# A two-layer decoder trunk: values first, the first weights loaded whole, and the forget gate's sums in six pieces

## The chip, the cores and the metric

The kernel runs on one core of a Trainium2 chip. Its engines are TensorE (PE, with weight loads listed apart as PEld), VectorE (DVE), ScalarE (ACT), GpSimd (POOL) and SyncE (SP), which here issues the DMAs. The metric is the device time of one execution in microseconds (us). Before the change it is 2600.77 us, the median of three runs (2596.73 to 2602.89).

## The reference

The input is 2048 tokens of width 1024, in float32. Layer A normalizes the tokens and projects them with one weight matrix of 4112 columns to q, k, v (1024 each), 16 forget logits and a gate. Cut to what matters here:

```python
u = rmsnorm(h, norm_a_g[i])
proj = u @ w_in_a[i]
q, k, v, f_logit, gate = jnp.split(proj, [...])
q = rmsnorm(q.reshape(b, s, 16, 64), qnorm_a_g[i])
k = rmsnorm(k.reshape(b, s, 16, 64), knorm_a_g[i])
log_f = jax.nn.log_sigmoid((f_logit + b_forget[i]).astype(jnp.float32))
c = jnp.cumsum(log_f, axis=1)
logits = q @ k.T * scale + c[query] - c[key]      # causal, per head
o = softmax(logits) @ v
h = h + (o * jax.nn.silu(gate)) @ w_out_a[i]
```

Layer B then computes one shared set of keys and values from h, projects its own q and gate, rotates 16 of 64 dimensions by angles that come from the token positions, attends in a window of 128 tokens, and adds its output projection. It is not touched by the change.

## The kernel before

Every float32 product is made of three matmuls: each operand is split into a high and a low part (`uh`, `ul` for the normed tokens, `wh`, `wl` for the weights), and high x high, high x low and low x high are summed in one accumulator. A token block is 128 tokens; with a contraction of 1024 = 8 x 128 a block and a group of columns take 24 matmuls, all on line 525.

Layer A's projections (`projections`) run over seven groups of columns, and within a group over 16 token blocks. The groups before are: q heads 0 to 5 with the 16 forget logits (400 columns), q heads 6 to 11 (384), k heads 0 to 7 and 8 to 15 (512 each), v heads 0 to 3 with q heads 12 to 15 (512), v heads 4 to 9 and 10 to 15 (384 each). The first group also norms the tokens (`norm`, `norm_transpose`: a load of x, squares on ACT, the reciprocal root on DVE, eight transposes on PE), two blocks ahead of their use. A block of q or k is then normed per head (`qk_norm`), transposed on PE a block or two later (`qk_transpose`), split, and stored for two blocks at a time. A block of v is split and stored at once (`v_tile`). The accumulators are three buffers `b2`; transposes use `pa` and `pb`.

A group's weights come by `weights`: four loads, each of two 128-row strips into one of two `wr` buffers, and eight splits (line 335 on ACT, line 336 on DVE) into nine buffers `wh` and nine `wl`. The x tiles of odd blocks use the same two `wr` buffers. The x tiles of even blocks, the stages of q and k, value tiles of over four heads and the gate-weight splits all take one of four buffers `st`.

Beside the blocks, 24 side jobs run, four to a group from the second group on (blocks 0, 3, 6, 9): 16 saves of the normed tokens to DRAM (`spill_u`, 1 MB each), then eight splits of the gate weights (`split_w`: a load of 512 KB, two splits, two stores; three `st` buffers). Attention needs both, since it computes the gate projection as filler between its own matmuls (line 785), with the saved tokens coming back through `wh` and `wl`. After its group, `forget` computes the log-sigmoid of the forget logits (exponential and logarithm on ACT), a running sum over all tokens (two matmuls, 15 small additions), and its transposed rows, stored as `ca`.

After the last group come the angle tables (`angles`, small operations on DVE and one sine on ACT) and attention. It goes head by head and, within a head, through four chunks of 512 queries. For each 128 queries it first finds row maxima (line 668, one or two pieces, each a matmul or two and a reduction on DVE), writes them by DMA as a row of the q operand, and then computes scores (lines 714, 715), exponentials on ACT, a high-low split on ACT and POOL, sums on DVE, and the product with v (line 755). The maxima of the next head are computed beside the scores of the current one; for the first head there is no earlier head to stand beside.

The program is written as loops, but the framework that builds it places each engine's instructions itself, by the readiness that it expects; the saves alone are held in program order. An engine, and SP with its DMA issues, then executes its list strictly in that order.

Of the kernel before, what the change touches and what calls it, by code (L numbers as in the profile page):

```python
# [21 lines left out]
P = 128  # L22
# [26 lines left out]
JOBS_AT = (0, 3, 6, 9)  # L49

# [22 lines left out]
class Trunk:  # L73
# [230 lines left out]
    def weights(self, src, c0, w, gain=None, extra=None, into=None):  # L304
# [9 lines left out]
        for dt in range(NDT):  # L314
            if dt % 2 == 0:
# [89 lines left out]
    def normer(self, src):  # L405
# [11 lines left out]
        def upto(n):  # L417
            while done[1] < min(n, NTB):
                while done[0] < min(done[1] + 2, NTB):
                    _, junk = parts(done[0])  # L420
                    ready.append(self.norm(src, done[0], junk))
                    done[0] += 1
                self.norm_transpose(ready.pop(0), *parts(done[1]))
# [4 lines left out]
    def projections(self, normed, groups, later=None, pre=None, hook=None):  # L428
# [7 lines left out]
        norm(1)  # L436
        if pre is not None:
            self.load_vectors(self.loads[:1])
        SW = 2 * P
        stages = {}  # L440
        z = None
# [13 lines left out]
        if later is not None:  # L455
# [23 lines left out]
            jobs = [  # L479
# [3 lines left out]
            jobs += [partial(split_w, dt) for dt in range(NDT)]  # L483

        for gi, grp in enumerate(groups):
            x2 = grp.get("extra")
            n = grp["n"] + (x2[1] if x2 else 0)
            W = self.weights(grp["w"], grp["c0"], grp["n"], grp["gain"], x2)
            if gi == 0:
                norm(2)  # L490
                if pre is not None:
                    pre()
# [24 lines left out]
            for tb in range(NTB):  # L517
                norm(tb + NORM_AHEAD)
                if gi and tb in JOBS_AT and jobs:
# [28 lines left out]
            if grp.get("forget"):  # L548
                self.forget(z)

    def forget(self, z):
# [3 lines left out]
        e, u = self.sb("sq", sh), self.sb("sq", sh)  # L555
        d, r = self.sb("qn", sh), self.sb("qn", sh)
# [10 lines left out]
        flat = r.rearrange("p t h -> p (t h)")  # L567
        inb, tot = self.ps("pa", sh), self.ps("pb", sh)
        nc.tensor.matmul(inb.rearrange("p t h -> p (t h)"), self.tri, flat, start=True, stop=True)
        nc.tensor.matmul(tot.rearrange("p t h -> p (t h)"), self.ones, flat, start=True, stop=True)  # L570
        nc.vector.memset(e[:, 0, :], 0.0)
        for tb in range(1, NTB):
            nc.vector.tensor_tensor(e[:, tb, :], tot[:, tb - 1, :], e[:, tb - 1, :], ALU.add)
        nc.vector.tensor_tensor(z, inb, e, ALU.add)
        sc = -float(HD) ** 0.5
        for ch in range(NCH):
            tr = self.ps(("pa", "pb")[ch % 2], [H, 4, P])
            for j in range(4):
                self.flip(tr[:, j, :], z[:, ch * 4 + j, :])
            trf = tr.rearrange("h j t -> h (j t)")  # L580
            hl = self.sb("st", [H, 2, CH])
# [609 lines left out]
```

## Time and profile before

| what | us |
|---|---|
| median of three runs | 2600.77 |
| the profiled execution | 2600.68 |
| its span in the trace | 2598.8 |
| first projection matmul | 11.7 |
| layer A's first group (400 columns, with the norms) | 11.7 to 114.1 |
| second group (384 columns, beside `forget`) | 114.1 to 195.3 |
| the two k groups | 195.3 to 387.9 |
| v with the last q heads | 387.9 to 479.7 |
| the two v groups | 479.7 to 616.1 |
| attention's first head | 616.1 to 699.3 |
| mean granted share of the TensorE clock | 0.983 |

A timeline row gives the start, the duration, the engine, the line, the operation, what it writes and reads, shapes and count, and in brackets the idle time of the engine ahead of it and what ended it. Matmuls are pipelined: a row's duration is longer than the distance to the next row, and the distance is what a stream of them costs. In a table of stretches a row gives from and to, the length, then the busy time and instruction count of each engine, the granted TensorE clock, the share of the DMA engines' time and GB/s.

### The profile page before, as it was taken

The page shows a single profiled execution, that of the slowest core. Times are in us where ns is not written, and L with a number is a line of the kernel's source. Part 1 is how long each engine was busy: PE and PEld are TensorE (multiplying, and loading weights), DVE is VectorE, ACT ScalarE, POOL GpSimd, SP SyncE. Part 2 cuts the span into 40 slices and gives each one's busy share as a digit, 9 for nine tenths or more (in the row PEclk, how much of TensorE's full clock was granted, in tenths as well). Part 3 has the DMA queues.
Part 4 walks back from the last instruction along what each step waited for, and adds up shares of the span by engine and source line. Part 5 has one row for each costly group of instructions (what it writes and reads, how often), then busy time and mean ns, then how long its engine had stood idle before and what let it go on. Part 6 is the DMA issues. An engine that isn't in the chain of part 4 may idle for free.

```text
span 2598.8 us, 37795 instructions
## 1 busy us (share of the span) xinstructions
PE 2506.7 (96%) x12412; PEld 2091.2 (80%) x12412; DVE 1678.5 (65%) x4140; ACT 1372.7 (53%) x2674; POOL 941.1 (36%) x611
## 2 busy tenths in 40 slices
PE   7999999999999999999999969999999999899999
PEld 7898888897777887878878747778888888688887
DVE  6765554424888888888878875446756401688885
ACT  5532322322777777777777772124422213677774
POOL 0000000011677777777777751200011000355543
PEclk9999999999999999999999979999999999899999
DMA  4545545677646655665664378864534523656652
GB/s 144 167 127 173 158 130 182 193 242 226 187 128 172 193 132 154 181 179 147 170 183 124 88 217 247 251 195 140 138 93 116 152 81 100 185 164 170 167 142 65
DMA packets 356547, 416.15 MB, mean 160 GB/s; under 512 B 65376, under 2 KB 251744, under 8 KB 350176
## 3 DMA queue, kind: packets, MB, share of 16 engines
q1 hardware_dynamic: 356352, 413.75, 55.5%
q8 instruction: 98, 1.61, 0.3%
q14 instruction: 97, 0.79, 0.1%
HBM read 262.13 MB, written 151.39 MB: 159 GB/s over the span
## 4 chain that ended last, share of the span: by engine, by line
PE 62%; DMA 7%; DVE 2%; ACT 1%; issue 1%; SPq 1%; POOL 0%; DVEq 0%; ACTq 0%; POOLq 0%
PE pa L755 9%; PE b L525 9%; PE pb L1052 7%; PE pb L785 7%; PE b L502 6%; PE sc L714 5%; PE mx L668 5%; PE sc L715 5%; PE b L265 2%; PE pa L1017 2%; DMA st<-rd 2%; PE b L913 2%; DMA h<-qn 2%; PE b L958 1%; PE b L961 1%
## 5 line engine op out<-in xcount | busy, mean ns | idle before, releaser
L525 PE MATMUL b<-wh,big 128*128 128x512 f32 (+2 forms) x2560 | 771.5, 375 | 6.5 <-ACT wh L335 2.6
L729 POOL TENSOR_TENSOR big<-st,big 128x1024 fp32r<-128x1024 f32 (+1 forms) x320 | 678.5, 2127 | 268.8 <-ACT big L728 161.1
L525 PEld LDWEIGHTS b<-wh,big 128*128 128x128 f32 x2560 | 476.8, 189 | 67.9 <-ACT wh L335 4.5
L525 PE MATMUL b<-wl,big 128*128 128x512 f32 (+2 forms) x1280 | 474.8, 371 | 0.6 <-DVE wl L336 0.6
L740 DVE TENSOR_TENSOR ac<-ac,st 128x512 f32<-128x512 f32 (+3 forms) x576 | 355.8, 618 | 80.6 <-ACT st L723 36.6
L755 PE MATMUL pa<-big 128*128 128x512 f32 (+2 forms) x1280 | 336.1, 375 | 13.4 <-POOL big L729 9.0
L723 ACT ACTIVATE st<-sc 128x512 f32<-128x512 f32 (+1 forms) x512 | 273.5, 583 | 113.1 <-PE sc L715 84.5
L728 ACT CAST big<-st 128x1024 fp32r<-128x1024 f32 (+1 forms) x320 | 301.8, 944 | 8.6
L755 PEld LDWEIGHTS pa<-big 128*128 128x128 f32 x1280 | 226.8, 191 | 57.2 <-POOL big L729 13.4
L525 PEld LDWEIGHTS b<-wl,big 128*128 128x128 f32 x1280 | 241.8, 189 | 32.3 <-DVE wl L336 4.0
L677 DVE CUSTOM_DVE_ANT_0 mx<-mx,rot 128x768 f32<-128x768 f32 (+11 forms) x256 | 225.1, 879 | 59.9 <-PE mx L668 58.6
L346 ACT ACTIVATE sq<-b 128x512 f32<-128x512 f32 (+2 forms) x128 | 66.3, 518 | 361.2 <-PE b L525 359.6
L714 PE MATMUL sc<-big 128*128 128x512 f32 (+2 forms) x640 | 248.8, 390 | 8.2 <-ACT st L723 7.3
L715 PE MATMUL sc<-big 67*128 67x512 f32 (+2 forms) x640 | 237.3, 372 | 0.0
L668 PE MATMUL mx<-big 66*128 66x320 f32 (+8 forms) x704 | 206.2, 367 | 4.1 <-DVE m L677 1.4
L348 DVE TENSOR_REDUCE sm<-sq 128x8 f32<-128x512 f32 (+2 forms) x128 | 75.0, 586 | 196.1 <-ACT sq L346 195.7
L785 PE MATMUL pb<-wh,wr 128*128 128x512 f32 x512 | 183.5, 400 | 1.9 <-DMA wr<-wg 1.3
L502 PE MATMUL b<-big,wh 128*128 128x512 f32 x512 | 159.9, 394 | 1.5 <-DVE mx L968 0.8
L987 POOL TENSOR_TENSOR st<-st,rs 128x1024 f32<-128x1024 f32 (+1 forms) x64 | 118.4, 1851 | 113.8 <-DVE rs L986 82.2
L596 POOL MEMSET big<- 3x2048 f32 x2 | 3.6, 1808 | 425.0 <-issue 425.0
L668 PEld LDWEIGHTS mx<-big 66*128 66x128 f32 x704 | 121.9, 193 | 41.9 <-DVE m L677 12.7
L714 PEld LDWEIGHTS sc<-big 128*128 128x128 f32 x640 | 124.4, 194 | 31.1 <-ACT st L723 10.8
(206 smaller groups left out, 4327.9 us busy)
## 6 DMA issues: line engine op xcount, KB each, us to landing
wr<-wg SPq DMA_DIRECT2D x64, 512.0 KB, 4.3
ut<-big SPq DMA_DIRECT2D x16, 1024.0 KB, 6.0
ka<-st SPq DMA_DIRECT2D x64, 256.0 KB, 4.0
big<-ka SPq DMA_DIRECT2D x16, 1024.0 KB, 6.5
big<-qa SPq DMA_DIRECT2D x16, 1024.0 KB, 7.4
qb<-st SPq DMA_DIRECT2D x64, 256.0 KB, 3.9
big<-qb SPq DMA_DIRECT2D x16, 1024.0 KB, 6.5
qa<-st SPq DMA_DIRECT2D x64, 192.0 KB, 3.2
```

The source lines that it names most:

```text
L502: nc.tensor.matmul(ps, W[k][dt][:, ft * P : (ft + 1) * P], u[ch][:, dt, :], start=(dt == 0 and i == 0), stop=(dt == NDT - 1 and i == 2),)
L525: nc.tensor.matmul(ps[:, :n], u[tb // 4][:, dt, us], W[k][dt], start=(dt == 0 and i == 0), stop=(dt == NDT - 1 and i == 2),)
L668: nc.tensor.matmul(ps[:, b, :wb], qb[:66, i * P : (i + 1) * P], kb[:66, k0 + b * wb : k0 + (b + 1) * wb], start=True, stop=True,)
L677: nc.vector.tensor_tensor_reduce(out=lg, in0=lg, in1=mask, scale=1.0, scalar=NEG, op0=ALU.add, op1=ALU.max, accum_out=f_(o),)
L714: nc.tensor.matmul(o, ka[:, ks], qa[:, qs], start=not (last and n_), stop=False)
L715: nc.tensor.matmul(o, kb[:, ks], qb[:, qs], start=False, stop=not diag)
L723: nc.scalar.activation(pf[:, off : off + w], ps[:, :w], AF.Exp, scale=HD**-0.5)
L728: nc.scalar.copy(ph[:, :tw], pf[:, :tw])
L729: nc.gpsimd.tensor_tensor(pl[:, :tw], pf[:, :tw], f_(ph[:, :tw]), ALU.subtract)
L740: nc.vector.tensor_tensor(a_, a_, pf[:, off : off + w], ALU.add)
L755: nc.tensor.matmul(pv[:, q0 : q0 + w], v[:, k, :], src[:, off : off + w], start=(p == 0 and n_ == 0 and i == 0), stop=(last and n_ == 1 an ...
L785: nc.tensor.matmul(ps, w[:, dt // 2 % 2, wk, dt % 2, :], us[dt][uk], start=(dt == 0 and i == 0), stop=(dt == NDT - 1 and i == 2),)
```

## The change

Three things change, all in layer A's projections.

The seven groups come in another order and with other borders: v heads 0 to 7 and 8 to 15 (512 columns each), k heads 0 to 7 and 8 to 15 (512 each), q heads 0 to 5 with the forget logits (400), q heads 6 to 11 (384), q heads 12 to 15 (256).

The first group's weights are loaded whole, into one `big` buffer of 16 KB per partition, by four loads that are issued after the first two x tiles; the splits read from there. The other small vectors are loaded at block 3. The side jobs change places: the eight gate-weight splits come first, the 16 saves after them.

`forget` no longer runs at once behind its group. It returns six pieces (log-sigmoid, running sum, and four of 512 tokens each that transpose, split and store), which run at blocks 1, 3, 5, 6, 7 and 8 of the group that follows. Its four intermediate tiles share one `st` buffer, its sums one `b2` buffer, its rows go through `wr`.

```diff
+VECTORS_AT = 3
+FORGET_AT = (1, 3, 5, 6, 7, 8)
...
         for dt in range(NDT):
-            if dt % 2 == 0:
+            if ahead is not None:
+                raws = ahead[:, dt // 2 * 2 : dt // 2 * 2 + 2, :]
+            elif dt % 2 == 0:
                 raws = self.sb("wr", [P, 2, CH])[:, :, :tw]
...
-        norm(1)
+        raw0 = None
         if pre is not None:
-            self.load_vectors(self.loads[:1])
+            raw0 = self.sb("big", [P, NDT, CH])
...
+            norm(1, [partial(load_raw, 0), partial(self.load_vectors, self.loads[:1])])
+            for dt in range(2, NDT, 2):
+                load_raw(dt)
+        else:
+            norm(1)
...
-            jobs = [
+            jobs = [partial(split_w, dt) for dt in range(NDT)]
+            jobs += [
                 partial(spill_u, ch, k, c0)
                 for ch in range(NCH) for k in range(2) for c0 in (0, NDT // 2)
             ]
-            jobs += [partial(split_w, dt) for dt in range(NDT)]
...
             for tb in range(NTB):
                 norm(tb + NORM_AHEAD)
+                if gi == 0 and tb == VECTORS_AT and pre is not None:
+                    pre()
+                if tb in FORGET_AT and forget:
+                    forget.pop(0)()
...
             if grp.get("forget"):
-                self.forget(z)
+                forget = self.forget(z)
+        for job in forget:
+            job()
...
+        t = self.sb("st", [P, 4, NTB, H])
+        e, u, d, r = (t[:, i] for i in range(4))
+        def logs():
+            self.log_sigmoid(z, e, u, d, r)
+        def running():
+            both = self.ps("b2", [P, 2, NTB, H])
...
+        def rows(ch):
...
+            hl = self.sb("wr", [H, 2, CH])
...
+        return [logs, running] + [partial(rows, ch) for ch in range(NCH)]
...
         groups = [
+            group(2 * D, 8, v=v_(0, 8)),
+            group(2 * D + 8 * HD, 8, v=v_(8, 8)),
+            group(D, 8, qk=k_(0, 8)),
+            group(D + 8 * HD, 8, qk=k_(8, 8)),
             group(0, 6, (3 * D, H), qk=q_(0, 6), forget=True),
             group(6 * HD, 6, qk=q_(6, 6)),
-            group(D, 8, qk=k_(0, 8)),
-            group(D + 8 * HD, 8, qk=k_(8, 8)),
-            group(2 * D, 4, (12 * HD, 4 * HD), v=v_(0, 4), qk=q_(12, 4, 4 * HD)),
-            group(2 * D + 4 * HD, 6, v=v_(4, 6)),
-            group(2 * D + 10 * HD, 6, v=v_(10, 6)),
+            group(12 * HD, 4, qk=q_(12, 4)),
         ]
```

In the changed program the line numbers are other ones: projection matmuls are on line 554, row maxima on 713, scores on 759 and 760, the product with v on 800, the gate filler on 830. From a point in attention's second head on, every engine's order is the one of before.

At the start of the program, SP's queue stands as follows before; `st` and `wr` are x tiles where `in_x` is read, `wr` is the first group's weights where `in_w_in_a` is read, and `g_a` to `gk` are small vectors.

```order
L286 DMA st<-in_x 128x1024
L286 DMA wr<-in_x 128x1024
L200 DMA g_a<-in_norm_a_g 128x8x1
L318 DMA wr<-in_w_in_a 128x2x384
L318 DMA wr<-in_w_in_a 128x2x16
L286 DMA st<-in_x 128x1024
L200 DMA bf<-in_b_forget 128x16
L200 DMA g_qa<-in_qnorm_a_g 64x1 x2
L200 DMA g_ka<-in_knorm_a_g 64x1 x2
L318 DMA wr<-in_w_in_a 128x2x384
```

And with the change:

```order
L289 DMA st<-in_x 128x1024
L289 DMA wr<-in_x 128x1024
L203 DMA g_a<-in_norm_a_g 128x8x1
L452 DMA big<-in_w_in_a 128x2x512 x4
L289 DMA st<-in_x 128x1024
L289 DMA wr<-in_x 128x1024 x2
L203 DMA bf<-in_b_forget 128x16
L203 DMA g_qa<-in_qnorm_a_g 64x1 x2
L203 DMA g_ka<-in_knorm_a_g 64x1 x2
L203 DMA g_b<-in_norm_b_g 128x8x1
L203 DMA g_kv<-in_kv_norm_g 128x8x1
L203 DMA g_qb<-in_qnorm_b_g 64x1
```

All four weight loads now stand ahead of the third x tile; before, one pair of strips stood there, and the second pair behind the vectors.

On ACT, the exponential and the logarithm of the forget gate (lines 559 and 564 before) stand between two groups: `wh` is a weight split of the next group, `sq` with a `b` the squares of a finished block.

```order
L335 ACTIVATE wh<-wr,g_a 128x384 x3
L374 ACTIVATE st<-pb,g_qa 128x3x128
L559 ACT_TABLE_LOAD
L559 ACTIVATE sq<-sq 128x256
L564 ACT_TABLE_LOAD
L564 ACTIVATE sq<-sq 128x256
L346 ACTIVATE sq<-b_1410 128x384
L346 ACTIVATE sq<-b_1447 128x384
L275 ACT_TABLE_LOAD
```

With the change they are lines 627 and 632:

```order
L352 ACTIVATE sq<-b_4001 128x384
L380 ACTIVATE st<-pb,g_qa 128x3x128
L278 ACTIVATE sm<-sm 128x6
L627 ACT_TABLE_LOAD
L627 ACTIVATE st<-st 128x256
L352 ACTIVATE sq<-b_4048 128x384
L632 ACT_TABLE_LOAD
L632 ACTIVATE st<-st 128x256
L278 ACT_TABLE_LOAD
```

The squares of a block now stand between the two.

On PE, where layer A's projections end and attention begins, the order before is this (`mx` row maxima, `sc` scores, `pb` gate filler):

```order
L525 MATMUL b_5616<-wh,big 128x384
L668 MATMUL mx<-big 128x128
L714 MATMUL sc<-big 128x512
L714 MATMUL sc<-big 128x384
L785 MATMUL pb<-wh,wr 128x512
L668 MATMUL mx<-big 128x256
L785 MATMUL pb<-wl,wr 128x512
L714 MATMUL sc<-big 128x256
L785 MATMUL pb<-wh,wr 128x512 x2
L668 MATMUL mx<-big 128x384
```

With the change:

```order
L554 MATMUL b_5508<-wh,big 128x256
L268 MATMUL pb<-ident,qn 128x128 x2
L268 MATMUL pa<-ident,qn 128x128 x2
L268 MATMUL pb<-ident,qn 128x128 x2
L713 MATMUL mx<-big 128x128
L713 MATMUL mx<-big 128x256
L713 MATMUL mx<-big 128x384
L713 MATMUL mx<-big 128x512
L713 MATMUL mx<-big 128x320 x2
L713 MATMUL mx<-big 128x384 x2
L713 MATMUL mx<-big 128x448 x2
L713 MATMUL mx<-big 128x512 x2
```

The transposes of the last q blocks stand at the handover, and a row of maxima follows; 13 pieces of maxima stand ahead of the first matmul of line 760, and the first gate filler comes some 85 rows further down, in the third chunk of the first head.

More of the change, by code (lines that the diff above doesn't have):

```diff
@@ L302, in norm_transpose, with weights @@
         nc.vector.tensor_tensor(ul, ps, f_(uh), ALU.subtract)
-    def weights(self, src, c0, w, gain=None, extra=None, into=None):
+    def weights(self, src, c0, w, gain=None, extra=None, into=None, ahead=None):
         nc = self.nc
@@ L415, in parts, with upto @@
             return (u[ch][:, :, t0 : t0 + P] for u in (uh, ul))
-        def upto(n):
+        def upto(n, loads=()):
+            loads = list(loads)
             while done[1] < min(n, NTB):
@@ L422, in upto @@
                     done[0] += 1
+                    if loads:
+                        loads.pop(0)()
                 self.norm_transpose(ready.pop(0), *parts(done[1]))
@@ L435, in projections, with load_raw @@
         norm, uh, ul = normed
-        norm(1)
+        raw0 = None
         if pre is not None:
-            self.load_vectors(self.loads[:1])
+            raw0 = self.sb("big", [P, NDT, CH])
+            def load_raw(dt):
+                g0 = groups[0]
+                nc.sync.dma_start(
+                    out=raw0[:, dt : dt + 2, :],
+                    in_=g0["w"][dt * P : (dt + 2) * P, g0["c0"] : g0["c0"] + CH].rearrange(
+                        "(k p) c -> p k c", p=P
+                    ),
+                )
+            norm(1, [partial(load_raw, 0), partial(self.load_vectors, self.loads[:1])])
[3 more added lines that the diff above has]
+            norm(1)
         SW = 2 * P
         stages = {}
-        z = None
+        z, forget = None, []
         def finish(q, qn, tb):
@@ L487, in projections @@
             n = grp["n"] + (x2[1] if x2 else 0)
-            W = self.weights(grp["w"], grp["c0"], grp["n"], grp["gain"], x2)
+            W = self.weights(
+                grp["w"], grp["c0"], grp["n"], grp["gain"], x2, ahead=None if gi else raw0
+            )
             if gi == 0:
                 norm(2)
-                if pre is not None:
-                    pre()
             if "gate" in grp:
@@ L566, in forget @@
         nc.vector.scalar_tensor_tensor(r, z, 0.0, u, ALU.min, ALU.subtract)
[L567 to L581, printed above, removed]
-            nc.scalar.activation(r_(hl[:, 0, :]), trf, AF.Copy, scale=sc)
-            nc.vector.scalar_tensor_tensor(
-                r_(hl[:, 1, :]), trf, sc, hl[:, 0, :], ALU.mult, ALU.subtract
-            )
-            nc.sync.dma_start(
-                out=self.d["ca"][:, :, ch * CH : (ch + 1) * CH].rearrange("k h t -> h k t"),
-                in_=hl,
-            )
     def attention_a(self):
```

27 lines of the change are left out of this document (25 added, 2 removed).

## The prediction

> **What bounds the kernel now.** I read the page first (TensorE has by far the most busy time), then a table of stretches cut at the borders of layer A's seven column groups (16 token blocks of 24 matmuls each) and at two points of the attention's first head behind them (the ends of its third and fourth chunk), then the timeline at the start, at the forget gate and where attention takes over.
>
> ```profile
> core 0: us, PE busy (x) PEld busy (x) DVE busy (x) ACT busy (x) POOL busy (x), PEclk, DMA share, GB/s
> 11.70:33.40 21.70, 15.60 (x67) 13.40 (x68) 13.98 (x48) 9.48 (x20) 0.00 (x0) 0.81 0.54 156
> 33.40:114.10 80.70, 77.99 (x475) 75.76 (x474) 63.14 (x200) 40.70 (x89) 0.00 (x0) 0.99 0.46 132
> 114.10:195.30 81.20, 77.52 (x453) 74.07 (x451) 50.84 (x166) 29.75 (x65) 1.25 (x2) 0.98 0.53 154
> 195.30:292.00 96.70, 95.94 (x454) 78.35 (x451) 49.79 (x137) 27.38 (x58) 0.00 (x0) 1.00 0.51 151
> 292.00:387.90 95.90, 95.38 (x451) 78.09 (x449) 49.84 (x136) 27.18 (x58) 0.00 (x0) 1.00 0.52 155
> 387.90:479.70 91.80, 91.80 (x420) 74.73 (x419) 44.46 (x151) 26.22 (x72) 0.00 (x0) 1.00 0.54 162
> 479.70:548.70 69.00, 67.42 (x390) 66.67 (x389) 23.37 (x56) 19.28 (x35) 0.00 (x0) 1.00 0.78 229
> 548.70:616.10 67.40, 67.18 (x385) 66.31 (x385) 16.01 (x24) 14.36 (x24) 7.07 (x4) 1.00 0.93 281
> 624.50:668.80 44.30, 39.95 (x155) 29.17 (x154) 31.09 (x56) 23.89 (x39) 23.57 (x12) 0.81 0.55 170
> 668.80:698.20 29.40, 29.30 (x141) 22.85 (x141) 25.84 (x49) 20.72 (x33) 21.35 (x11) 1.00 0.65 198
> ```
>
> TensorE bounds it, and a busy PE is not a fast one: what a stretch loses shows only against the spacing of undisturbed matmuls, which the timeline gives for the four widths concerned (512, 384, 400, 256 columns):
>
> ```profile
> 470.46 0.39 PE L525 MATMUL b<-wl,big 128*128 128x512 f32 x1
> 473.19 0.39 PE L525 MATMUL b<-wl,big 128*128 128x512 f32 x1
> 485.03 0.34 PE L525 MATMUL b<-wl,big 128*128 128x384 f32 x1
> 489.19 0.33 PE L525 MATMUL b<-wl,big 128*128 128x384 f32 x1
> 51.54 0.52 PE L525 MATMUL b<-wh,big 128*128 128x400 f32 x2
> 54.78 0.52 PE L525 MATMUL b<-wh,big 128*128 128x400 f32 x2
> 2299.94 0.28 PE L958 MATMUL b<-big 128*128 128x256 f32 x1
> 2300.78 0.28 PE L961 MATMUL b<-big 128*128 128x256 f32 x1
> 50.20 0.27 PE L265 MATMUL pb<-ident,qn 128*128 128x128 f32 x1
> 50.31 1.04 PE L265 MATMUL b<-ident,st 128*128 128x128 f32 x8
> 51.10 0.42 PE L525 MATMUL b<-wh,big 128*128 128x400 f32 x1
> ```
>
> Twelve matmuls lie between the first two rows (0.2275 us each), 24 between the next two (0.1733), 18 between the next (0.18), 7 in the 256-wide pair (0.12, with a weight load for each). A block of 24 so needs 5.46, 4.16, 4.32 or 2.88 us. One q or k transpose adds 0.11 (50.20 to 50.31), the eight of a normed token block 0.85 (0.79 seen at 50.31 to 51.10, plus the switch back). That makes the seven groups before: 86.3 (16 x (4.32+0.33) + 14 x 0.85), 71.8, 94.4, 94.4, 90.9, 66.6, 66.6, in all 571.0 us. They took 11.7 to 616.1, 604.4 us. **The loss is 33.4 us**: 16.1 in the first group, 9.4 in the second, 2.3 and 1.5 in the k groups, 0.9, 2.4 and 0.8 in the rest.
>
> **The change, part by part.** The reordering by itself: the new widths are 512, 512, 512, 512, 400, 384, 256, and the same sum gives 99.3 (two norms ahead, 14 inside), 87.4, 94.4, 94.4, 74.4, 71.8, 49.6, in all 571.3. Matmul count and columns are the same, so this costs 0.3 us. Only the last group could break the line, since a 128-column weight load is recorded with 0.19 us; but the 256-wide rows above step at 0.12 with a load each, so I take that, and keep 16 x 24 x 0.05 = 20 us out of the range.
>
> Start. Now:
>
> ```profile
> 8.38 1.15 ACT L335 ACTIVATE wh<-wr,g_a 128x400 fp32r<-128x400 f32 x2 [0.50 <-DMA wr<-in_w_in_a]
> 11.09 0.90 SPq L318 DMA_DIRECT2D wr<-in_w_in_a  x2
> 14.81 1.15 ACT L335 ACTIVATE wh<-wr,g_a 128x400 fp32r<-128x400 f32 x2 [2.11 <-DMA wr<-in_w_in_a]
> 33.45 0.68 PE L525 MATMUL b<-wh,big 128*128 128x400 f32 x1
> ```
>
> The second weight pair is issued only at 11.09, when a buffer of x comes free, and the third block starts at 33.45. Changed, four loads of 512 KB leave SP right behind g_a, from about 2.2 us. With the two x tiles that is 3 MB; at the 281 GB/s of the table's fullest stretch, from about 2.8 us on, the last lands near 13.5, or 16 if it goes a fifth slower. The eight splits (about 0.7 on ACT and on DVE each) then end near 16.5 and the first block near 18. The x tiles of blocks 2 and 3 queue behind the weights; squared, scaled and transposed they let the second block start at about 21 and the third at 27.7. The ideal from 11.7 would be 24.4, so 4 us stay lost with the first matmul's delay, 0.5 more in the rest of the group, where no qk chain remains: 11.6 won here. On SP's queue the load of x for the fifth block now stands behind the first value store and six vector loads (0.45 us an issue, as at 11.09): out at about 23, landed 3.7 later (11.09 to 14.81), normed near 32 and needed near 33; the later ones go two blocks ahead of their use. That cover is 1 us; without it the group slips by what is missing, once. For the vectors themselves nothing waits before group 3.
>
> Forget gate. Now its chain stands between two groups on every engine:
>
> ```profile
> 121.21 1.28 ACT L559 ACT_TABLE_LOAD   x1
> 128.22 0.67 PE L569 MATMUL pa<-qn,tri 128*128 128x256 f32 x2 [1.57 <-DVE qn L566]
> 132.85 0.44 PE L525 MATMUL b<-wh,big 128*128 128x384 f32 x1 [1.78 <-DVE qn L351]
> 494.52 0.41 PE L525 MATMUL b<-wh,big 128*128 128x384 f32 x1 [1.18 <-DVE st L392]
> ```
>
> PE's own part (two sums, 16 small transposes) is some 3 us and stays. In pieces, the other 5 us lie under blocks of 4.5 us, and PE has three accumulators (`b2`), so two blocks' time, before it must wait; three table loads like the one at 121.21 remain on ACT, which is busy 29.75 of 81.2 us there. I leave 1 us of stall and 1.1 for the border: 9.4 becomes 5.1, 4.3 won.
>
> Borders and side jobs. Each group border costs about 1.1 (1.5 + 0.9 + 0.8 in the three quiet groups of the table, and the same elsewhere); five others stay, 5.5. The gate weight splits now share the four `st` buffers with full-width value tiles and then with k stages (two buffers each), where before they met value tiles of 384 columns only and cost 1.18 once (494.52). I put 1.4 there and 1.5 in the first k group, bounded by 0 and by 1.2 for each of eight splits, 9.6. The saves of u move from groups 2 to 5 into 4 to 7, where the gate splits were (0.78 and 0.93 DMA share, with no more than 2.4 us lost); like sizes take their place, and I add nothing. In all the changed losses are 4.5 + 5.1 + 5.5 + 2.9 = 18.0; layer A's projections then end at 11.7 + 571.3 + 18.0 = 601.0 instead of 616.1: **15.1 us won**.
>
> The handover is where something is given back. Before, a value group came last and attention followed without a gap:
>
> ```profile
> 616.10 0.22 PE L668 MATMUL mx<-big 66*128 66x128 f32 x1
> 622.02 0.56 PE L668 MATMUL mx<-big 66*128 66x320 f32 x2 [0.38 <-DVE m L677]
> 624.49 0.40 PE L715 MATMUL sc<-big 67*128 67x512 f32 x1
> 625.30 0.70 PE L668 MATMUL mx<-big 66*128 66x448 f32 x2
> 698.68 0.64 PE L755 MATMUL pa<-big 128*128 128x256 f32 x4
> 39.50 0.56 DVE L348 TENSOR_REDUCE sm<-sq 128x6 f32<-128x384 f32 x1 [3.39 <-ACT sq L346]
> 41.53 0.56 DVE L351 TENSOR_TENSOR qn<-b,sm 128x384 f32<-128x384 f32 x1
> 628.76 1.05 PE L668 MATMUL mx<-big 66*128 66x512 f32 x2
> 660.84 0.63 PE L668 MATMUL mx<-big 66*128 66x512 f32 x2
> ```
>
> ```profile
> L241 DVE TENSOR_SCALAR cossin<-qn x1: 229/229/229, 508.9 to 508.9; 128x128 f32<-128x128 f32 x1
> ```
>
> Now q heads come last: PE must wait for the last block's norm (2.6 us from 39.50 to the end of 41.53, 0.5 for the squares ahead of it) and transpose it, some 4 us. PE's new order then has 13 row-maximum pieces (1.64 us each: two between 622.02 and 625.30; the four small ones about 1.0) before the first completed scores, with no gate matmuls between. 4 + 9 x 1.64 + 4 = 23 us lie between the last projection and the first scores, against 8.4 (624.49). The angle tables' 16 small DVE operations (3.7 us at 0.229 each) and the Sin table move into this stretch too, in DVE's gaps between pieces. In return the maxima of later chunks are ready early, and by the end of the third chunk, and of the head, both orders have issued the same gate matmuls (24, and 52). From the first scores to the end of the third chunk the new order has 157 matmuls; at the rate of the fourth chunk (141 in 29.4 us) that is 33, so 56 from the last projection on, against 668.8 - 616.1 = 52.7. The fourth chunk is as before. I take **3.3 us lost**, between a gain of 3 (the small and middle pieces a fifth faster, undisturbed by scores) and the whole delay of 14.6; PE-bound work being equal, it is nearer to the former.
>
> The clock column shows 0.81 here: one pair of 512-wide matmuls took 1.05 us at 628.76 and 0.63 at 660.84. With all 13 pieces at the slower rate (7744 columns, 7.6 such pairs x 0.42) 3.2 us would come on top. A rule says that they will be: the Trainium skill ("TensorE: Matmul & The Clock Gate", "Why this matters for your kernels") has the array fall to half its clock where gaps of more than about 3 us part bursts of matmuls; the trace agrees in the row at 628.76. By that rule the sum below would be 2592.1 instead of 2588.9. I leave the 3.2 out, since PE mostly waits for DVE between pieces, and keep it for the range.
>
> Sum on the profiled execution (2600.68 us, span 2598.8, 1.9 around it): -15.1 + 3.3 = -11.8, so 2588.9. The median shown is 2600.77, 0.09 higher: **2589**.
>
> **Rivals.** (1) The handover costs nothing: PE-bound heads follow, with equal gate work. 2585.6, or 2582.6 with its gain of 3. For it: POOL and DVE were busy only 23.57 and 31.09 of 44.3 us in 624.5 to 668.8. (2) Buffers: the splits stall value and key groups at the upper bound, 9.6 instead of 2.9: 2595.6. For it the 1.18 at 494.52; against it two blocks, 11 us, of slack. (3) The weights land no sooner than the DMA lets them, and the second block starts at 26 instead of 21: 2594. (4) The other side: the first head is one chain from its first scores on, so all of the 14.6 shift, with 3.7 of angle work in the same DVE queue and 3.2 of half clock: 21.5 lost against 15.1 won, 2607. It decides from a shift of 15.1 on. Against it: that chain was also waiting for maxima, which now come first.
>
> **How the numbers follow.** Forecast 0.50, rival 1 0.20, rival 2 0.13, rival 3 0.08, rival 4 0.09. About 0.2% (5.2 us) is what a measurement of this kernel tells from no change. Faster, below 2595.6: 0.46 of the forecast, rival 1, 0.06 of rival 3, a little of 2: 0.75. Slower, above 2606: 0.08 of rival 4. Same: 0.17. The range runs from the handover's gain of 3 with the first three blocks at their ideal (2578.6) to the whole delay of 14.6 with some of rival 2 (2600.2 and up).
>
> **What would show it.** Right: third block's first matmul near 28 us; second group without a stretch of forget work; first attention maxima (now line 713) near 604, first completed scores (760) near 624, the first head's end near 687 instead of 698.7. Wrong: second block later than 25, blocks over 6.5 us in the second and third group behind `wg<-st`, 256-wide blocks slower than 3.3, or a first head longer than 97 us (82.6 now, and 15.1 more), which would eat the gain.

## The result and the profile after

The changed kernel takes 2610.14 us (median of 13 runs, 2605.11 to 2618.71), the kernel before 2600.77 (13 runs beside it). The ratio is 1.0041, 95% interval 1.0031 to 1.0051: slower by 0.4%, where 2589 was forecast. The profiled execution of the changed kernel took 2605.39 us (span 2603.4), so it lies 4.7 us under the median; a second one (below) shows what a more usual execution adds. One run of v_last and one of gate_act0 below took over 9000 us, in a slow state; the ratios rest on the other runs, which by themselves have medians of 2589.10 and 2604.76.

The table of stretches of the changed kernel: seven rows for the groups of layer A's projections, then the first head of attention, cut at the first completed scores, at the end of its third chunk and at its own end. Columns as before.

```profile
12.20:120.90 108.70, 104.03 (x496) 86.44 (x497) 52.48 (x129) 45.58 (x80) 0.00 (x0) 0.98 0.50 149
120.90:208.70 87.80, 87.60 (x386) 71.92 (x385) 21.89 (x28) 19.49 (x28) 0.00 (x0) 1.00 0.63 193
208.70:303.20 94.50, 94.48 (x446) 77.70 (x444) 52.04 (x131) 30.35 (x58) 0.00 (x0) 1.00 0.57 165
303.20:398.90 95.70, 95.29 (x450) 78.04 (x449) 49.35 (x136) 26.93 (x58) 0.00 (x0) 1.00 0.52 152
398.90:473.70 74.80, 74.80 (x435) 73.81 (x434) 44.29 (x151) 22.80 (x57) 0.00 (x0) 1.00 0.55 167
473.70:554.70 81.00, 78.33 (x455) 74.70 (x454) 49.94 (x166) 29.29 (x66) 1.24 (x2) 0.98 0.50 149
554.70:604.34 49.64, 49.64 (x418) 49.47 (x417) 35.31 (x132) 16.98 (x52) 7.10 (x4) 1.00 0.73 211
604.34:630.60 26.26, 12.48 (x33) 7.08 (x30) 15.20 (x50) 3.49 (x7) 0.00 (x0) 0.57 0.73 199
630.60:668.43 37.83, 36.92 (x163) 28.78 (x162) 27.05 (x45) 28.39 (x46) 24.59 (x13) 0.89 0.58 182
668.43:700.10 31.67, 28.52 (x135) 21.39 (x135) 25.44 (x50) 18.10 (x30) 20.69 (x10) 1.00 0.57 152
```

The projections do end earlier, 604.3 instead of 616.3. The first head then takes 95.8 us (604.34 to 700.10) instead of 83.0 (616.26 to 699.3), with the same matmuls (33 + 163 + 135 recorded; 25 + 157 + 146 before, cut at the same events). In its first 26 us TensorE is busy 12.48, at a granted clock of 0.57. The same stretch of the kernel before, where gate filler stood between the maxima:

```profile
616.26:624.49 8.23, 5.88 (x25) 3.61 (x23) 3.86 (x12) 1.76 (x2) 0.00 (x0) 1.00 0.87 276
```

The whole first head in the changed kernel (first row) and before (second row), then the changed kernel's head cut where the clock changes (two rows), and the two parts of the head before that ran at half clock:

```profile
604.34:700.10 95.76, 77.92 (x328) 57.25 (x326) 67.70 (x145) 49.97 (x81) 45.28 (x22) 0.84 0.62 177
616.26:699.30 83.04, 76.25 (x324) 56.71 (x323) 61.86 (x118) 47.44 (x76) 45.23 (x22) 0.90 0.61 188
607.90:638.50 30.60, 18.96 (x48) 12.01 (x47) 16.69 (x47) 7.88 (x12) 2.97 (x2) 0.50 0.58 155
638.50:668.43 29.93, 29.84 (x142) 23.45 (x140) 23.21 (x40) 22.68 (x37) 21.62 (x12) 1.00 0.68 210
625.80:632.60 6.80, 6.18 (x18) 4.56 (x17) 3.04 (x6) 2.64 (x5) 3.32 (x2) 0.50 0.61 190
649.70:659.90 10.20, 9.54 (x23) 7.16 (x24) 5.86 (x9) 5.81 (x10) 4.76 (x2) 0.50 0.93 315
```

Over the head TensorE idles 17.8 us (95.76 - 77.92) instead of 6.8 (83.04 - 76.25): 11.0 of the 12.7 us that the head is longer.

What TensorE does in the first 26 us (the timeline of PE):

```profile
604.40 0.38 PE L268 MATMUL pa<-ident,qn 128*128 128x128 f32 x2
607.73 0.41 PE L268 MATMUL pb<-ident,qn 128*128 128x128 f32 x2 [2.94 <-DVE qn L357]
615.58 1.01 PE L713 MATMUL mx<-big 66*128 66x384 f32 x2 [0.98 <-DVE m L722]
617.70 1.12 PE L713 MATMUL mx<-big 66*128 66x448 f32 x2 [1.12 <-DVE m L722]
620.07 1.22 PE L713 MATMUL mx<-big 66*128 66x512 f32 x2 [1.25 <-DVE qn L224]
630.60 0.63 PE L760 MATMUL sc<-big 67*128 67x512 f32 x1
653.03 0.50 PE L830 MATMUL pb<-wh,wr 128*128 128x512 f32 x1
```

First comes the wait for the last block's norm, then one piece of row maxima after the other. PE waits for DVE before each, DVE for PE, and a full-size piece takes 2.1 to 2.4 us (615.58 to 617.70 to 620.07). The first gate filler (line 830) stands at 653.03, 49 us behind the last projection; before, it stood between the maxima from 617.7 on. In PE's order it stands that late; SP's queue shows that its inputs could not have been there much sooner:

```profile
605.22 6.01 SPq L388 DMA_DIRECT2D qa<-st  x8
611.91 1.59 SPq L665 DMA_DIRECT2D big<-qa  x1
614.92 10.37 SPq L405 DMA_DIRECT2D big<-m  x8
625.34 0.58 SPq L820 DMA_DIRECT2D wh<-ut  x1
646.25 0.43 SPq L826 DMA_DIRECT2D wr<-wg  x1
```

Eight q stores, the loads of head 0, eight row stores that wait for the maxima, then the filler's saved tokens from 625.34 and its weights at 646.25.

From the second head on the order of every engine is the one of before, and the difference stays nearly flat, with one step. Here the gate weights come late, by 2.44 us, in a place where PE waited 0.54 before (the first row is of the changed kernel, the second of the kernel before):

```profile
1006.28 0.50 PE L830 MATMUL pb<-wh,wr 128*128 128x512 f32 x1 [2.44 <-DMA wr<-wg]
```

```profile
1002.54 0.50 PE L785 MATMUL pb<-wh,wr 128*128 128x512 f32 x1 [0.54 <-DMA wr<-wg]
```

Behind the wait the clock falls (0.65 granted from 1008 to 1012, where the kernel before has 1.00). Over this place the changed kernel falls back by 3.5 us (1.8 behind before it, 5.3 after it, at the same sums). Layer B starts at 1761.15 instead of 1754.28 and wins 2.2 back.

### The profile page after: what moved, and what is told of

It reads as the page before. It is cut to its first block, busy times and chain, and to the rows that moved or that the text cites. A ratio compares the mean times of both kernels' runs of the same rounds, so it can differ in the third digit from the quotient of the medians.

```text
span 2603.4 us, 37663 instructions
## 1 busy us (share of the span) xinstructions
PE 2507.1 (96%) x12412; PEld 2078.4 (80%) x12412; DVE 1679.7 (65%) x4124; ACT 1372.3 (53%) x2658; POOL 939.8 (36%) x611
## 4 chain that ended last, share of the span: by engine, by line
PE 83%; DMA 7%; DVE 4%; ACT 3%; issue 1%; SPq 1%; POOL 0%; DVEq 0%; ACTq 0%; POOLq 0%
PE b L554 28%; PE pa L800 9%; PE pb L830 7%; PE b L527 6%; PE pb L1097 6%; PE mx L713 5%; PE sc L759 5%; PE sc L760 5%; PE b L268 3%; PE pa L1062 2%; DMA h<-qn 2%; DMA st<-rd 2%; PE b L958 2%; PE b L1003 1%; PE b L1006 1%
## 5 line engine op out<-in xcount | busy, mean ns | idle before, releaser
L554 PE MATMUL b<-wh,big 128*128 128x512 f32 (+3 forms) x2560 | 768.3, 376 | 3.2 <-DVE st L602 2.0
L554 PE MATMUL b<-wl,big 128*128 128x512 f32 (+3 forms) x1280 | 475.1, 372 | 0.5 <-DVE wl L342 0.5
L800 PEld LDWEIGHTS pa<-big 128*128 128x128 f32 x1280 | 228.4, 192 | 51.7 <-ACT sq L808 11.9
```

Of the source, the lines that this page charges most:

```text
L554: nc.tensor.matmul(ps[:, :n], u[tb // 4][:, dt, us], W[k][dt], start=(dt == 0 and i == 0), stop=(dt == NDT - 1 and i == 2),)
L800: nc.tensor.matmul(pv[:, q0 : q0 + w], v[:, k, :], src[:, off : off + w], start=(p == 0 and n_ == 0 and i == 0), stop=(last and n_ == 1 an ...
```

## The experiments

Times are medians; beside each stands the difference to the runs of the kernel before on the same chip. "First head" is from the last projection matmul to the last product with v of head 0.

**v_last.** One line moved:

```diff
             group(2 * D, 8, v=v_(0, 8)),
-            group(2 * D + 8 * HD, 8, v=v_(8, 8)),
             group(D, 8, qk=k_(0, 8)),
...
             group(12 * HD, 4, qk=q_(12, 4)),
+            group(2 * D + 8 * HD, 8, v=v_(8, 8)),
```

> The changed kernel with one line moved: value heads 8 to 15 stand last again, behind the q groups. Theory (handover): with q last, the gate loads stand on SP's queue behind the last q stores and the row loads, so the first head's maxima run without filler, and 13 us are lost between the last projection and the second head. With a value group last the gate filler should stand between the maxima again, the first head should take about 83 us as before (96 now), and the time should be 2610 - 13 = 2597 (2593 to 2600). Rival A (the loss is spread: late gate loads all through attention, other buffers): the first head improves little, 2606 to 2612. Rival B (the values-first start and the pieces are worth nothing in the whole program): like before, 2600 to 2602.

2589.19 us, ratio 0.9948 (0.9935 to 0.996): 12.5 us faster than before, 21 faster than the change with the same start, pieces and side jobs, and 4 below the range that was expected. The first head takes 76.8 us, where 83 was expected. Its table, cut at the same events, and its SP queue:

```profile
605.78:613.81 8.03, 5.71 (x26) 3.80 (x24) 3.86 (x12) 1.87 (x2) 0.00 (x0) 1.00 0.79 239
613.81:656.90 43.09, 40.49 (x179) 29.31 (x179) 31.73 (x58) 23.77 (x39) 24.24 (x12) 0.96 0.63 206
656.90:682.60 25.70, 24.73 (x121) 18.84 (x120) 22.26 (x40) 19.03 (x31) 19.68 (x9) 1.00 0.39 102
```

```profile
602.97 1.06 SPq L820 DMA_DIRECT2D wh<-ut  x1
607.77 2.78 SPq L405 DMA_DIRECT2D big<-m  x3
610.65 0.54 SPq L820 DMA_DIRECT2D wh<-ut  x1
```

The saved tokens are loaded from 601.2 on, beside the last value stores, and later stand between the row stores. First scores come 8.0 us behind the last projection, and the clock stays at 0.96 to 1.00. That is where this head beats the one before too: it was at half clock for 3.4 us instead of 17.0, which by the estimate further down is worth 5.5 of the 6.2 us. The step near 1000 us is there too (3.0 us), so it does not belong to the handover.

**order_back.** The seven groups of before, with the new start, pieces and side jobs (the extra columns of the first group are loaded into the same buffer).

> The changed kernel with the seven groups in the order and widths of before; the whole first weights (now 400 columns, vectors loaded at block 0), the pieces and the swapped side jobs stay. Handover theory: the first head is as before, and what the start wins is kept: 2600.8 - 6.7 (the first group lost 9.4 instead of 16.1 us) = 2594 (2590 to 2597). Rival B: the start is only a shift that later waits take back, 2600 to 2602. Rival A (loads that come late in attention whenever the saves run last): 2600 to 2606.

2594.36 us, ratio 0.998 (0.9967 to 0.9993): 7.4 faster than before, as the handover reading said. The start and the pieces are worth something in the whole program, and the new order alone turns that into a loss. The step near 1000 us is absent.

**gate_act0.** Only the loads of the first chunk's filler, on another queue:

```diff
-nc.sync.dma_start(out=f_(us[dt][k]), in_=d["ut"][ch, k, dt])
+(nc.sync if ch else nc.scalar).dma_start(out=f_(us[dt][k]), in_=d["ut"][ch, k, dt])
```

(and the first gate weights likewise)

> The changed kernel; only the first chunk's gate loads (16 loads of the saved tokens, the first gate weights) are issued from ACT's queue instead of SP's. The order of groups stays. Handover theory: the loads no longer stand behind the row loads, filler stands between the first maxima, and a good part of the 13 us comes back: 2600 to 2605, the first head at 86 to 91 us. Rival C (the chain of maxima on DVE and the norm of the last q block set the handover, whatever the filler does): first scores still come 26 us behind the last projection and, since the filler is not what PE lacks, 2608 to 2612.

2605.46 us, ratio 1.0017 (1.0003 to 1.0031): 3.7 over before instead of 9.4, more than half of the loss back. Filler now stands between the maxima, but two new waits stand there too (the table of waits):

```profile
DVE qn L224 <- DMA sq<-in_positions: 5.6, 1, 5.6
ACT sm L278 <- DMA wh<-ut: 2.6, 1, 2.6
```

On ACT the last norm stands behind a load that waits for its buffer; on DVE the maxima stand behind the angle work, which waits for the positions. Both are side effects of the edit, so three more trials followed.

**angles_early, both_early, gate_pool0.** The angle tables in the fourth group (`if pre is not None and gi == 3 and tb == 13: self.angles()`); that and the filler's first loads from POOL's queue (`nc.gpsimd` for `nc.scalar` above); the loads alone.

> The changed kernel with the angle tables (load of the positions, 16 operations on DVE, one sine) computed in the fourth group instead of behind the last one. Theory E (the angle work stretches the bare maxima of the handover): the 3.7 us of DVE work and the table load leave it, 2605 to 2607. Handover theory, in which missing filler is what PE lacks: the order of maxima ahead of the scores stays, so at most 1 to 2 us, 2608 to 2611.

> As angles_early, and the first chunk's gate loads (saved tokens and first gate weights) issued from POOL's queue, which has nothing else to do there, instead of SP's; this is the trial with ACT's queue without its side effects (there the last norm on ACT stood 2.6 us behind a gate load, and a maximum on DVE 5.6 us behind the positions). Handover theory: filler stands under the maxima without holding any engine, 9 to 13 of the 13 us come back, 2597 to 2602. Rival C (the chain of the last q norm, its stores, the loads of head 0 and the maxima sets the end of the first head): not below 2604.

> The changed kernel, with the first chunk's gate loads from POOL's queue and nothing else (both_early without the angles). Handover theory: the loads are what counts, 2599 to 2602 like both_early. Rival F (the filler only helps once the angle work has left DVE and the positions' load has left SP): 2604 to 2609, as with ACT's queue.

angles_early: 2610.33 us, ratio 1.0045 (1.0032 to 1.0059), nothing won. both_early: 2599.78, ratio 0.9999 (0.9989 to 1.0008). gate_pool0: 2600.04, ratio 0.9998 (0.9987 to 1.0009). So where the 18 filler loads stand is worth some 10 us, and the angle work nothing that can be seen, alone or together with it. In both_early first scores still come 25.7 us behind the last projection; what changed is that filler stands under the maxima. The first 25 us of the head, in the changed kernel and in both_early:

```profile
604.10:629.10 25.00, 11.97 (x32) 6.56 (x30) 14.61 (x50) 3.49 (x7) 0.00 (x0) 0.58 0.72 194
602.50:627.50 25.00, 17.68 (x76) 12.27 (x73) 12.11 (x35) 2.75 (x8) 7.45 (x14) 0.83 0.94 329
```

(The profiled execution of gate_pool0 was one of its longest, 2605.4 in span; no reading is taken from its stretches.)

**k_last.** The k groups behind the q groups: a normed group is last, but not the q heads.

> The changed kernel with the two k groups moved behind the q groups: a normed group is still last, but the q rows of head 0 are long stored and filler stands between the maxima in PE's order, as before the change. Handover theory (what counts is where the filler's loads stand): the norm of the last block costs its 4 to 5 us, the rest comes back, 2594 to 2600. Rival G (any normed group at the end costs the 13 us, through its eight stores on SP's queue and the chain behind them): 2606 to 2612.

2603.11 us, ratio 1.0012 (1.0001 to 1.0022): 2.8 over before and so between the two readings, some 7 better than the change and 15 worse than v_last. SP's queue there:

```profile
602.73 0.37 SPq L820 DMA_DIRECT2D wh<-ut  x1
606.73 7.68 SPq L388 DMA_DIRECT2D ka<-st  x8
614.51 12.65 SPq L405 DMA_DIRECT2D big<-m  x8
627.25 0.54 SPq L820 DMA_DIRECT2D wh<-ut  x1
```

Three of the eight pairs of saved tokens pass ahead of the last stores; the others stand behind stores and rows again. That is a partial handover in the sense of v_last, and it does not separate the norm from the queue. The next edit leaves the norm and moves only stores:

**store_pool.** Only the stores of the last group from POOL's queue; the filler's loads stay on SP.

```diff
+                    nc.gpsimd if q["dst"] is self.d["qa"] and q["p0"] == 6 else None,
```

> The changed kernel with the stores of its last group (32 stores of q heads 12 to 15) issued from POOL's queue; everything else, the gate loads too, stays on SP. In PE's order this puts gate filler between the first maxima again. Handover theory in its narrow form (the last group's stores hold up, on SP, the loads of head 0, the row stores and the gate loads): of the 13 us all but the wait for the last norm (4 us) come back, 2599 to 2603. Rival G (the norm of the last block and the bare chain of maxima on DVE are the cost, whatever is queued): 2606 to 2611.

2602.78 us, ratio 1.0013 (1.0003 to 1.0022): 2.8 over before, so 6.6 of the 9.4 us of loss are gone with 32 stores off SP's queue. First scores come 15.0 us behind the last projection instead of 26.3, and the norm's wait of 2.6 is still there:

```profile
606.73 0.28 PE L555 MATMUL b<-wh,big 128*128 128x256 f32 x1
610.56 0.44 PE L268 MATMUL pb<-ident,qn 128*128 128x128 f32 x2 [2.61 <-DVE qn L357]
611.89 0.63 PE L831 MATMUL pb<-wh,wr 128*128 128x512 f32 x1
622.04 0.40 PE L761 MATMUL sc<-big 67*128 67x512 f32 x1
```

In gate_act0, both_early, gate_pool0 and store_pool alike the framework answered the edit with another order on PE, in which filler stands between the first maxima. So the runs show what the place of these transfers is worth together with the order that follows from it. What the queue alone would hold up, with PE's order unchanged, no run shows.

**forget_once, forget_before.** First the six pieces at once behind their group, in their new buffers; then the function of before in its old buffers.

```diff
-                forget = self.forget(z)
+                for job in self.forget(z): job()
```

> The changed kernel with the forget gate's six pieces run at once behind their group, as before the change. By the forecast the pieces won 4.3 us, so 2614 to 2615. Rival, from the changed trace, where the group with the pieces takes 81.0 us against an ideal of 71.8 (9.2 lost; 9.4 before): the pieces won nothing, 2609 to 2611.

> The changed kernel with the forget function of before, run at once behind its group with its old buffers; the earlier trial put the pieces at once behind the group, and there the weights of the next group waited for the rows in the buffers they share. Forecast: the pieces won 4.3 us, so 2614. Rival, from the two traces, where the group behind it lost 9.4 before and 9.2 now: nothing won, 2609 to 2611. If it is as slow as the earlier trial (2637), the shared buffers were not the cause.

2636.87 and 2611.87 us (ratios 1.0133 and 1.0054). The first is outside both expectations; it only shows a price of the new buffers: the rows take `wr`, and the next group's weights wait for them.

```profile
476.49 6.53 SPq L388 DMA_DIRECT2D qa<-st  x8
495.51 4.48 SPq L617 DMA_DIRECT2D ca<-wr  x4
500.73 7.01 SPq L324 DMA_DIRECT2D wr<-in_w_in_a  x4
```

The second is the true undoing: 11.9 us over before, ratio 1.0054 (1.0038 to 1.0071), against 9.4 and 1.0041 (1.0031 to 1.0051) with the pieces. The intervals overlap, and the changed kernel itself was 12.3 over in its second set of runs (after_again below), so no gain by the pieces can be told here. In the two traces the group behind the forget gate takes 79.8 us without the pieces and 81.0 with them.

**v_last_vec, v_last_pvec, after_pvec.** The start. In the changed kernel 11.2 us instead of 6.34 lie between the first matmuls of the third and the fourth block (the expectations below call this stretch the fourth block), since the x tile of the fifth block, whose transposes stand there, is squared late; SP issues that tile behind six vector loads that follow the first store:

```profile
22.70 0.59 SPq L203 DMA_DIRECT2D g_qb<-in_qnorm_b_g  x1
26.72 0.43 SPq L289 DMA_DIRECT2D st<-in_x  x1
33.73 1.06 ACT L291 ACTIVATE big<-st 128x1024 fp32r<-128x1024 f32 x1 [4.54 <-DMA st<-in_x]
```

v_last_vec sets `VECTORS_AT = 14`; v_last_pvec and after_pvec issue the vectors from POOL's queue (`self.load_vectors(self.loads[1:], nc.gpsimd)`), with v_last's order and with the change's.

> As v_last, with the small vectors loaded at block 14 of the first group instead of block 3, behind all x tiles. In v_last the fourth block of the first group took 10.58 us and the fifth 7.95 where 6.34 is the usual. Theory (vectors): the x tile of the fifth block is issued behind the vector loads (26.72 in the changed kernel, squared from 33.73 on), so both blocks return to about 6.4, the first group takes 103 instead of 108.8 us, and the time is 2589.2 - 5.8 = 2583 (2581 to 2586). Rival D (the x tile is late because of weights and first stores, whatever the vectors do): the fourth block stays above 9 us, 2588 to 2590.

> As v_last, with the small vectors loaded from POOL's queue. The earlier trial moved them in the program text alone, and the framework left them where they were on SP's queue (22.93 to 26.96, ahead of the x tile of the fifth block), so it tested nothing. Theory (vectors): without them SP issues that x tile right behind the first value store, near 23 instead of 26.96, and the fourth block (10.5 us) and the fifth (7.96) lose 4 to 5.8 us together: 2588 - 5 = 2583 (2581 to 2586). Rival D (the transfer itself is late, or POOL's small loads slow it the same): the fourth block above 9 us, 2586 to 2590. Beside it: a step of about 3 us near 1000 us, where one gate-weight load comes late, in the changed kernel and v_last and not before; if it hangs on the position in SP's queue, it moves or goes here.

> The changed kernel with the small vectors loaded from POOL's queue. If the start's shortfall is what it was in the other order, 5 to 6 us less than the changed kernel: 2604 to 2605. If the step near 1000 us goes with it (it fell from 3 to 1 us when the same edit was made to v_last), 2 us less again: 2602.

v_last_vec: 2586.07 us, ratio 0.9949 (0.9937 to 0.9961). The stretch still takes 10.5 us, and SP issues the vectors where it did: the framework placed the loads by its own reckoning. As an experiment on the vectors it is void, as a repetition of v_last it gives the same ratio. v_last_pvec: **2580.93 us, ratio 0.9926 (0.9909 to 0.9943), faster than both kernels**. The x tile goes out right behind the first store, and the stretch takes 6.34 us:

```profile
25.25 0.38 SPq L399 DMA_DIRECT2D va<-st  x1
25.67 0.58 SPq L289 DMA_DIRECT2D st<-in_x  x1
```

The first matmul comes 3.6 us later there (15.6 instead of 12.0; the splits waited for the weights), so the first group ends at 118.9 instead of 120.8, and the projections end at 603.4 instead of 605.9. By the third head nearly all of that is gone: at the same sums v_last_pvec stands at 764.39, v_last at 764.94 and v_last_vec at 764.34. So it is luck that 2580.93 lies near the forecast of 2583. The repaired start is not what makes v_last_pvec shorter in these traces; most of the difference arises at the step near 1000 us and behind the last sums but one, where profiles of one kernel differ too, and its interval overlaps with those of v_last and v_last_vec. after_pvec: 2605.95 us, ratio 1.003 (1.0016 to 1.0043), 6.0 over before instead of 9.4; in its trace 4.2 us are won at the end of the projections, and 1.3 are left in the third head. The step near 1000 us shrank to 1.0 in v_last_pvec but is 3.3 in after_pvec, so the guess that it hangs on the length of SP's queue falls.

**v_last_pool.** v_last_pvec, and the filler's first loads from POOL's queue.

> As v_last_pvec, and the first chunk's gate loads from POOL's queue too: the handover of v_last with its filler loaded earlier. The first head of v_last takes 77 us, of which TensorE still idles or runs slow some 8. Theory: 1 to 4 us less than v_last_pvec, 2580 to 2583. Rival: the filler is early enough with a value group last, the same as v_last_pvec within 1.

2595.0 us, ratio 0.9976 (0.9965 to 0.9986): 14 slower than v_last_pvec by the differences to before, against both expectations. In the first 25 us of the first head TensorE is busy 18.9 us at a clock of 0.75, in v_last_pvec 20.4 at 0.93. The queue on which a load stands is no free choice. What costs it there was not isolated, since PE's order changed with it.

**after_again.** The changed kernel, once more.

> The changed kernel unchanged, for a second profile: its profiled execution lay 4.7 us below the median of its runs. The time should be 2608 to 2612; if the span is near the median, the extra lies where the executions of the other kernels differ too, in the last part of attention and the output projection (252 to 262 us from the last sums to layer B), and not in the handover, which should take 26 us to the first scores again.

2612.26 us, span of the profile 2609.4, of which 6.0 more than the first profile. The first group, the projections' end and the step near 1000 us are as they were. First scores come 26.5 us behind the last projection, as expected. The extra is 3.5 us in the first two heads, where none was expected, and 3.0 between the last sums but one and layer B, where it was. Most of the 3.5 is the clock: it was at half for 37.5 us of the first head here (607.3 to 641.4 and 682.4 to 685.8) and for 30.6 in the first profile, an estimated 2.8 us more by the working below. In all the profiles of this study the stretch from the last sums but one to layer B took 253 to 262 us, whatever the edit.

## Why the prediction was wrong

The working, step by step, against the profile of the changed kernel:

| step | predicted | measured |
|---|---|---|
| ideal of the widths, 256 columns above all | 49.6 for the last group | 49.64 |
| loss of the first group | 4.5 | 9.4 (108.7 - 99.3) |
| loss of the group with the pieces | 5.1 | 9.2 (81.0 - 71.8) |
| other borders and splits | 8.4 | 2.2 (0.4 + 0.1 + 1.3 + 0.4 + 0.0) |
| end of the projections | 601.0 | 604.3 |
| last projection to first completed scores | 23 | 26.3 |
| from there to the end of the third chunk | 33 | 37.8 |
| fourth chunk | as before, 30 | 31.7 |
| behind the first head, to the end | 0 | 3.8 (from 0.8 to 4.6 behind the kernel before) |

**The step that failed** is the handover, "3.3 us lost, between a gain of 3 and the whole delay of 14.6; PE-bound work being equal, it is nearer to the former". The profiled execution lost 12.7 in the first head. The order was read rightly: 13 pieces ahead of the first scores of line 760, the first filler some 85 rows down. The prediction's three terms for the head, 23 + 33 + 30, came to 86 us; it took 95.8.

The term that was mis-sized most is the clock. The 33 goes by the rate of a stretch at clock 1.00, and the 3.2 us for the half clock were left out. The clock was granted at half from 607.9 to 638.5, across the first two terms; behind that, 142 matmuls took 29.9 us, which is about the predicted rate (141 in 29.4). What it cost is an estimate: 512 columns step at 0.43 us at half clock (638.12 to 638.55 in the trace) and at 0.23 at full (639.12 to 639.35), and the matmuls that start in those 30.6 us have 33 times 512 columns, so 6.6 us. Six matmuls more than counted in the second term (163, 157) make 1.3, and the fourth chunk 1.7, with TensorE idle for 3.1 us of it.

The clock is not what sets the two kernels apart, though. The kernel before was at half clock for 17.0 us of its first head, with 35.6 times 512 columns in them: 7.1 us by the same estimate. What sets them apart is the idle time, 17.8 us against 6.8. The prediction counted on PE-bound work behind the bare maxima to make up for it. First scores came 18.0 us later than before, and 12.7 of them were still missing at the end of the head. The filler that ran under the waits of the maxima before was moved behind them; while the maxima ran bare nothing replaced it. What I did not follow was SP's queue: I counted what PE does, not when the filler's inputs could be there. v_last and order_back show that the handover sets the sign; gate_pool0, both_early and store_pool show that moving transfers off SP's queue, with the order on PE that follows from it, wins 7 to 10 us back while the last norm, whose wait is 2.6 to 2.9 us, stays where it is.

**Rival 4** (2607, "all of the 14.6 shift, with angle work and half clock") comes nearest in size, to 0.1%, and had a chance of 0.09. Its mechanism is only partly right, so the nearness is partly luck: the angle work, 3.7 of its 21.5, was worth nothing, and the half clock weighed on the kernel before as well. That the handover is one chain which shifts as a whole is refuted by both_early: first scores as late as in the changed kernel, and 10 us less. Rival 1 (the handover costs nothing) is refuted by the 12.7.

**The clock's rule**: the table of stretches shows 0.57 and 0.89 where it was 1.00 and 0.81 before. The Trainium skill ("TensorE: Matmul & The Clock Gate", "Why this matters for your kernels") expects the fall from gaps over about 3 us. In the changed kernel one gap of 2.94 us stands at its head, and it stays low through gaps of 0.6 to 1.4, so in these 26 us bare maxima did not bring it back. In the kernel before it fell at 625.8 although no gap of TensorE since the last projection was longer than 0.98 us (at 623.56). So here it fell without a long gap, and the measurement decides: the prediction's "the trace agrees in the row at 628.76" holds for the half rate of that row and not for the gap. The reason for leaving the 3.2 out, that PE waits for DVE between pieces, was wrong: PE's own time stands in the same chain.

**The start** went as predicted up to the third block (27.9, predicted 27.7). Then the cover of 1 us for the x tile of the fifth block was not enough: 7.0 us passed from its issue to its squares (26.72 to 33.73) instead of the 3.7 taken, and the fourth block slipped by 4.9. The prediction had named that place, not its size. Won: 6.7 instead of 11.6.

**The forget gate** in pieces: 4.3 won predicted, nothing measurable found. The sums take one of three accumulators, and PE waits 1.99 us behind them; then 384-wide matmuls step at 0.32 us instead of 0.17 for some 3 us. Each piece of rows adds some 0.6 us to its block (a step of 0.72 to 0.78 instead of 0.17).

```profile
491.54 0.41 PE L554 MATMUL b<-wh,big 128*128 128x384 f32 x1 [1.99 <-DVE st L602]
```

**Borders and splits** cost 2.2 instead of 8.4: full-width value blocks give the four `st` buffers all the time they need. Rival 2 (9.6 there) is refuted by the second and third row of the table of stretches (87.8 and 94.5 us, ideals 87.4 and 94.4); rival 3 (late weights) in the changed kernel by the third block's time. Together the projections won 12 instead of 15; this alone would have left the forecast inside its range.

**Still open** is the step near 1000 us: 1.9 of its 3.5 us is the longer wait for one gate-weight load (2.44 instead of 0.54), and the lower clock behind it (0.85 over 2 us, 0.65 over 4) is worth an estimated 1.7. One row store ahead of that load took 1.83 us to issue in the changed kernel and 0.55 before, and no run shows why. The step is absent in order_back, 1.0 to 2.1 us in v_last_pvec, both_early, v_last_pool and gate_act0, and 2.6 to 4.4 in the rest.

## What to carry to other kernels

At the border of two phases, follow every queue that the next phase's first instructions depend on, the DMA issuer's above all: here an edit that put stores last also put the next phase's loads behind them. An engine that alternates with another engine in small pieces needs independent work between them, and that work's inputs must be issued ahead of the border. A rate taken from a stretch at full clock does not hold for one that runs at half. The order of phases is better judged by what the last one leaves undone than by what the first one gains: here a group without a norm and with one store per block belongs at the end, and moving one line was worth 21 us.

## What the runs showed of the hardware

The queue that issues a transfer mattered here, in both directions. The Trainium skill ("DMA: Bandwidth & Descriptors", "Rules for kernel authors") holds that spreading DMAs over issuing engines saves only the sequencer's issue time, since all use the same 16 engines. Here that time contains the waits that stand in the queue (eight row stores held SP for 10.37 us), and moving 32 stores or 18 loads off SP was worth 7 and 10 us in the changed kernel, and the same 18 loads on POOL's queue made v_last_pvec 14 us slower, each time with another order on PE.

The stretch from the last sums but one of attention to layer B took 253 to 262 us in kernels that do the same work there, and two profiles of the changed kernel differ by 3.5 us in the first two heads, mostly by how long the clock stayed at half (37.5 and 30.6 us). A single profile of the whole program thus decides nothing below some 4 us, and the medians above are what the verdicts rest on.
